# Two norms of the second layer whose sums of squares are taken later among the products

## The chip, the core and the metric

The kernel runs on one core of a Trainium2 chip. A core has engines that each work through a queue of their own in order and wait for one another by semaphores: TensorE (PE in the profile, with its weight loads as PEld) multiplies matrices into PSUM, VectorE (DVE) and ScalarE (ACT) do elementwise work, GpSimd (POOL) has very little to do here, and SyncE (SP) issues the transfers. The metric is the device time of one execution in microseconds (us); lower is better.

## What is computed

Two layers of a hybrid trunk over 256 latent tokens (LAT) with 256 context tokens (CTX), model width 1024. Cut to what the change touches:

```python
for l in range(DEPTH):                      # DEPTH = 2
    h  = modulate(rmsnorm(x,  norm1_g[l]), sh1, sc1)      # first norm, latent half
    hc = modulate(rmsnorm(xc, norm1_g[l]), csh1, csc1)    # first norm, context half
    p  = h @ w_in[l]                        # GLU columns, q, k, v, gates
    ...                                     # conv branch, attention, gated merge
    x  = x + g1 * gated_merge(...)
    h2 = modulate(rmsnorm(x, norm2_g[l]), sh2, sc2)       # second norm
    x  = x + g2 * conv_ffn(h2, w_up[l], ffn_dw[l], ffn_dw_b[l], w_down[l])
```

In the last layer (l = 1) the context gives only keys and values, and the feed-forward part runs over the latent tokens alone.

## The kernel before, in words

Activations lie with channels on the 128 partitions: `x[k]`, k = 0..7, is 128 channels by 512 tokens (256 latent, 256 context). Every weight tile of 128x1024 is fetched by a transfer (`raw`), split by ScalarE into a high part (`whi`, L160) and by VectorE into the rest (`wlo`, L161), with four buffers of each. A product of one weight tile is `mm3`: three matmuls, high weight by high activation (L179), high by low (L180), low by high (L181). One accumulation group is eight such triples, 24 matmuls, into one PSUM bank; there are two banks `sc`, four `main`, one `pt` and one `po`.

**A norm** has these steps. After each residual add (`x`, L898) the new `x[k]` is squared (ScalarE, L318) and added to a running sum `ss` (VectorE, L322). When all eight are in, TensorE sums `ss` over the partitions (`rstd`, L336, into `pt`); VectorE scales the result (`red`, L344); GpSimd raises it to the power -0.5 (`rs`, L346); TensorE spreads `rs` over the partitions (L351, into `po`). Then `modulated` runs for each k: VectorE multiplies x by gain and `po` (L365), ScalarE adds the shift and rounds to the high part (`h`, L366), and VectorE makes the low part (`h`, L367).

**Slots.** Side work is written as generators kept in a list; `slot()` is called between groups of matmuls and lets each generator take one step. `norm(..., rest)` is such a generator: it first rests for `rest` slots, then does L336 and `red` in one slot, waits one slot, does L351 and k = 0, 1 in the next, and two more k in each slot after that. A slot therefore sets where L336 and L351 stand in TensorE's queue; a scheduler then orders the other engines' queues by it.

**The first norm of layer 1** is made in two halves at the end of layer 0's down-projection: the latent half first, then the context half, with `rest` 1. The slots in which the context half runs are those at the start of layer 1: two per GLU weight tile (two tiles, banks `sc`), then one after each of the two groups of `glu_groups(1)` (banks `main`), then one after every second k of the V products (L644). V's first half uses the latent tokens, its second half is the first reader of the context half.

**The second norm of layer 1** does not run as side work. The four first up-projection tiles are multiplied by the un-normalised activations (258 columns: 256 tokens and two shift columns), row by row: row k is four tiles by three matmuls, 12 matmuls into banks `sc`, `sc`, `main`, `main`. Between rows, the code takes the first step of `sums` (L336, `red`, `rs`) and then the rest of it (L351). After row 7 `modulated` is written for all k, `po` is copied (`rstd1`, L1010), and the four products are multiplied by it (`u`, L1015), which frees their banks. The up-projections that follow are pairs i = 2..21, each two groups of 24 matmuls over the normalised `h2`, and each followed by `ffn_out`, which on VectorE is L964, L967 (twice each), L979 and L990.

Of the kernel before, what the change touches and what calls it, by code (L numbers as in the profile page):

```python
# [34 lines left out]
BADA, N1G, DW, DWB, LNG, LNB, N2G, FDW, FDB, NPAR = 0, 48, 56, 180, 184, 188, 192, 200, 332, 376  # L35
# [10 lines left out]
def trunk(ctx: ExitStack, tc: tile.TileContext, xt, cvec, crow, wall, wada, params, bias_t, rope_t, out):  # L46
# [19 lines left out]
    def psum(tag="main"):  # L66
        return psp.tile([P, 512], F32, tag=tag, bufs=BANKS[tag], name=nm(tag))
# [4 lines left out]
    def small(shape, tag, bufs=2):  # L72
        return tp.tile(shape, F32, tag=tag, bufs=bufs, name=nm(tag))
# [7 lines left out]
    def add_side(gen):  # L81
        side.append(gen)

    def slot():
        for g in list(side):
            try:
                next(g)
            except StopIteration:
                side.remove(g)

    def whole(g):

        while True:
            try:
                next(g)
            except StopIteration as e:
                return e.value

    def finish(g):
        for _ in g:  # L100
            pass
        if g in side:
            side.remove(g)
# [66 lines left out]
    def wunit(l, u, at=None, cuts=1):  # L170
        w, more = wparts(l, u, at, cuts)
        more()
        return w

    def cols(w, i):
        return sl(w[0], i), sl(w[1], i)

    def mm3(ps, w, xh, xl, start, stop):
        pe.matmul(ps, w[0], xh, start=start, stop=False)  # L179
        pe.matmul(ps, w[0], xl, start=False, stop=False)  # L180
        pe.matmul(ps, w[1], xh, start=False, stop=stop)  # L181
# [107 lines left out]
    def gain(l, part, off, k, ns=2):  # L289

        if (l, part) not in gains:
            gains[l, part] = cp.tile([P, KD, 2], F32, name=f"gain{l}_{part}")
        a = gains[l, part][:, k, :ns]
        g = pr(l, off + k, 1).to_broadcast([P, ns])
        dve.scalar_tensor_tensor(a, mod2(l, part, k)[:, :ns], 1.0, g, ALU.add, ALU.mult)
# [29 lines left out]
    def sum_squares(n, T, apart=False):  # L325

        at = tp.tile([P, 512], F32, tag="ss", name=nm("ss"))
        return [SumSq(T, at[:, i * T : (i + 1) * T], apart) for i in range(n)]

    def rstd(ss, n, bank):  # L330

        nt = ss.T // P
        pt = psum("pt")
        for i, p in enumerate(ss.parts):
            for t in range(nt):
                pe.matmul(  # L336
                    pt[:, t : t + 1], sl(p, t), one, start=i == 0 and t == 0, stop=i == len(ss.parts) - 1,
                    skip_group_check=True,
                )
        return (yield from root(pt, nt, n, bank))  # L340
# [13 lines left out]
    def h_tiles():  # L354
        return [[hp.tile([P, 2 * S + 2], F32R, tag=f"h{i}{k}", name=nm("h")) for k in range(KD)] for i in range(2)]

    def modulated(l, pb, scale, shift, k, h, streams):

        hi, lo = h[0][k], h[1][k]
        y = tmp()  # L360
        for s in streams:
            c = slice(s * S, (s + 1) * S)
            o = (s - streams[0]) * S
            a, b = gains[l, scale][:, k, s : s + 1], mod(l, shift, k, s)
            dve.scalar_tensor_tensor(y[:, c], x[k][:, c], a, pb[:, o : o + S], ALU.mult, ALU.mult)  # L365
            high = act.activation(hi[:, c], y[:, c], AF.Identity, bias=b)  # L366
            low = dve.scalar_tensor_tensor(lo[:, c], y[:, c], b, hi[:, c].bitcast(F32), ALU.add, ALU.subtract)  # L367
        return high, low

    def norm(l, acc, scale, shift, goff, h, streams, rest=0):  # L370
        for _ in range(rest):
            yield
        pb = yield from rstd(acc, D, "po")
        for k in range(KD):
            if streams[0] == 0:
                gain(l, scale, goff, k, 1 if l == DEPTH - 1 and scale == 4 else 2)
        for k in range(KD):
            modulated(l, pb, scale, shift, k, h, streams)
            if k % 2:
                yield  # L380
# [175 lines left out]
    h1 = h_tiles()  # L556

    for l in range(DEPTH):
# [5 lines left out]
        with ExitStack() if last else start as e1a:  # L564
# [68 lines left out]
            with ExitStack() as e1b:  # L633
# [98 lines left out]
                else:  # L732
                    sp.dma_start(rope, rope_t)
                    pg0 = [psum("sc") for _ in range(2)]
                    for uu in range(2):
                        wg = wunit(l, U_GLU0 + uu)
                        for i in range(2):
                            for kk in range(4):
                                k = 4 * uu + kk
# [76 lines left out]
            with ExitStack() as e1c:  # L816
# [79 lines left out]
                def residual(ss_, ps, part, n, s, off):  # L896
                    c = slice(s * S, (s + 1) * S)
                    dve.scalar_tensor_tensor(x[n][:, c], ps[:, off : off + S], mod(l, part, n, s), x[n][:, c], ALU.mult, ALU.add)  # L898
                    ss_.add(x[n][:, c], n == KD - 1)
# [19 lines left out]
                sss = sum_squares(NS, S)  # L919
# [15 lines left out]
                for s in range(NS if held else 0):  # L935
# [8 lines left out]
                    if s == 0:  # L944
                        finish(g1)
                        nl = norm(l, sss[0], 4, 3, N2G, h2, (0,))
# [3 lines left out]
        with ExitStack() as e2:  # L950
            ef = e2.enter_context(tc.tile_pool(name=f"ef{l}", bufs=1))
            if not last:
                finish(nl)
                nl = norm(l, sss[1], 4, 3, N2G, h2, (1,))
# [41 lines left out]
            if last:  # L996

                with tc.issue_after(lastev[0].ins):
                    act.activation(small([P, 1], "mx"), one, AF.Silu)
                for k in range(KD):  # L1000
                    for w, ps in zip(first, pss):
                        mm3(ps[:, : S + 2], w[k], h2[0][k][:, RAW], h2[1][k][:, RAW], k == 0, k == KD - 1)
                    if k == 2:
                        next(sums)
                    if k == 4:
                        pb = whole(sums)
                for k in range(KD):
                    modulated(l, pb, 4, 3, k, h2, (0,))
                rb = ef.tile([P, 512], F32, name="rstd1")
                act.copy(rb[:, LAT], pb[:, LAT])  # L1010
                for i, ps in enumerate(pss):
                    b = small([P, 1], "wb", 4)
                    act.copy(b, ps[:, S : S + 1])
                    u = ef.tile([P, S], F32, name=f"u{l}_{i}")
                    dve.tensor_tensor(u, ps[:, LAT], rb[:, LAT], ALU.mult)  # L1015
                    act.activation(u, u, AF.Identity, bias=b)
                    pss[i] = u
            else:
                for k in range(KD):
                    for w, ps in zip(first, pss):  # L1020
                        mm3(ps[:, LAT], w[k], h2[0][k][:, LAT], h2[1][k][:, LAT], k == 0, k == KD - 1)
                    slot()
                finish(nl)
# [29 lines left out]
            if not last:  # L1053
                h1 = h_tiles()
            sss = sum_squares(NS, S, last)
# [7 lines left out]
            for streams, ns in [((0, 1), range(NB)), *(((s,), range(NB, KD)) for s in range(NS))]:  # L1063
                wu = None
                c = slice(streams[0] * S, (streams[-1] + 1) * S)
                for n in ns:
                    ps = psum()
                    for k in range(KF):
                        t = n * KF + k
                        if t % 8 == 0 or not wu:  # L1070
                            wu = wunit(l, U_DN + t // 8)
                        mm3(ps[:, c], cols(wu, t % 8), fh[k][:, c], fl[k][:, c], k == 0, k == KF - 1)
                        if k % 4 == 3:
                            slot()
                    for s in streams:
                        residual(sss[s], ps, 5, n, s, s * S)
                    if last:
                        scaled = act.mul(x[n][:, CTX], x[n][:, LAT], par[:, DEPTH * NPAR + n : DEPTH * NPAR + n + 1])
                        if n == KD - 2:
                            with tc.issue_after(scaled.ins):  # L1080
                                act.activation(small([P, 1], "wb", 4), one, AF.Sqrt)
                if not last and streams == (0,):
                    finish(ad)
                if not last and len(streams) == 1:
                    nl = norm(1, sss[streams[0]], 1, 0, N1G, h1, streams, streams[0])
                    add_side(nl)


# [136 lines left out]
```

## Time and profile before

| | |
|---|---|
| median of 3 runs | 1131.16 us (1129.35 to 1134.31) |
| profiled execution, its own time | 1129.86 us |
| span of that execution, first to last instruction | 1128.1 us |
| mean granted TensorE clock | 0.997 |
| moved by transfers | 190.83 MB, mean 169 GB/s |

The difference between the span and the execution's own time, 1.8 us, lies around the first and the last instruction. In the tables of the profile, times are in us from the span's start; the two matmuls of L336 are listed there as four rows ("x4"). A bracket at the end of a timeline row is the idle time of that engine just before the row and what ended it. The TensorE clock and DMA share in the last columns of the table of windows are shares of full.

### The profile page before, as it was taken

What the parts mean: (1) busy time and instruction counts of PE and PEld (TensorE: products, weight loads), DVE (VectorE), ACT (ScalarE), POOL (GpSimd) and SP (SyncE); (2) the same over time, 40 slices, a digit from 0 to 9 for tenths busy, and PEclk for the clock granted to TensorE, in tenths of its full rate; (3) what the DMA queues carried; (4) which work ended last, traced back from release to release, by engine and by line L of the source; (5) the groups of instructions that cost most, each with busy time, mean ns of one, the idle gap of its engine ahead of it and who ended that gap; (6) DMA issues with size and microseconds to landing.
All of it is one profiled execution on the core that took longest, in us unless ns stands there. A gap on an engine that the chain in (4) does not pass through costs nothing.

```text
span 1128.1 us, 17731 instructions
## 1 busy us (share of the span) xinstructions
PE 1113.2 (99%) x6828; PEld 963.1 (85%) x6828; DVE 909.4 (81%) x1631; ACT 563.3 (50%) x934; POOL 17.2 (2%) x24
## 2 busy tenths in 40 slices
PE   9999999999999999999999999999999999999997
PEld 6778777787789988888888888989898999999997
DVE  5689999685778788888898555789996898988773
ACT  4347657542333543434443223444677567766642
POOL 0000000000000000000000000000000000000000
PEclk9999999999999999999999999999999999999998
DMA  9823231636734344554556655545433575565771
GB/s 361 283 94 104 75 117 38 205 97 217 245 114 144 114 154 149 168 172 146 172 171 218 224 185 189 175 174 175 153 121 115 181 240 172 187 194 180 217 269 57
DMA packets 53941, 190.83 MB, mean 169 GB/s; under 512 B 6240, under 2 KB 6496, under 8 KB 53856
## 3 DMA queue, kind: packets, MB, share of 16 engines
q1 hardware_dynamic: 53568, 189.65, 51.6%
q8 instruction: 54, 0.88, 0.3%
q14 instruction: 31, 0.25, 0.1%
q10 hardware_dynamic: 288, 0.04, 0.0%
HBM read 188.62 MB, written 1.05 MB: 168 GB/s over the span
## 4 chain that ended last, share of the span: by engine, by line
PE 84%; DVE 10%; DMA 3%; ACT 2%; issue 1%; SPq 0%; DVEq 0%; ACTq 0%
PE main L179 25%; PE main L181 24%; PE main L180 24%; DVE cb L591 4%; PE main L644 4%; DVE wlo L161 2%; DMA raw<-in_wall 1%; PE sc L179 1%; PE sc L181 1%; PE sc L180 1%; PE po L202 1%; PE po L512 1%; DMA x<-in_xt 1%; DMA sb<-in_crow 0%; PE sc L440 0%
## 5 line engine op out<-in xcount | busy, mean ns | idle before, releaser
L179 PE MATMUL main<-h,whi 128*128 128x256 f32 (+1 forms) x1328 | 447.5, 338 | 0.0
L181 PE MATMUL main<-h,wlo 128*128 128x256 f32 (+1 forms) x1328 | 444.0, 335 | 0.5 <-DVE wlo L161 0.5
L180 PE MATMUL main<-h,whi 128*128 128x256 f32 (+1 forms) x1328 | 443.0, 334 | 0.0
L160 ACT CAST whi<-raw 128x1024 fp32r<-128x1024 f32 (+1 forms) x244 | 252.4, 1039 | 286.0 <-PE main L180 127.3
L161 DVE TENSOR_TENSOR wlo<-raw,whi 128x1024 fp32r<-128x1024 f32 (+1 forms) x244 | 293.5, 1209 | 113.9 <-ACT whi L160 107.3
L179 PEld LDWEIGHTS main<-h,whi 128*128 128x128 f32 x1328 | 249.8, 188 | 31.8 <-issue 3.9
L181 PEld LDWEIGHTS main<-h,wlo 128*128 128x128 f32 x1328 | 250.0, 189 | 28.7 <-DVE wlo L161 0.7
L180 PEld LDWEIGHTS main<-h,whi 128*128 128x128 f32 x1328 | 250.3, 189 | 27.9 <-issue 0.2
L591 DVE SCALAR_TENSOR_TENSOR cb<-u,par,cb 128x512 f32<-128x512 f32 (+1 forms) x240 | 140.4, 617 | 1.2
L271 DVE CUSTOM_DVE_ANT_0 t<-raw,sb,par 128x1024 bf16<-128x1024 f32 x100 | 126.8, 1279 | 1.0 <-ACT sb L255 0.8
L180 PE MATMUL main<-fl,whi 128*128 128x256 f32 (+1 forms) x386 | 123.1, 319 | 0.0
L179 PE MATMUL main<-fh,whi 128*128 128x256 f32 (+1 forms) x386 | 123.1, 319 | 0.0
L181 PE MATMUL main<-fh,wlo 128*128 128x256 f32 (+1 forms) x386 | 123.1, 319 | 0.0
L180 PEld LDWEIGHTS main<-fl,whi 128*128 128x128 f32 x386 | 72.8, 189 | 5.6
L181 PEld LDWEIGHTS main<-fh,wlo 128*128 128x128 f32 x386 | 72.8, 189 | 5.5
L179 PEld LDWEIGHTS main<-fh,whi 128*128 128x128 f32 x386 | 72.8, 189 | 5.5
L963 ACT ACTIVATE t<-main,par 128x512 f32<-128x512 f32 (+1 forms) x82 | 50.6, 668 | 40.0 <-PE main L181 39.8
L964 DVE SCALAR_TENSOR_TENSOR t<-main,par,t 128x510 f32<-128x510 f32 (+1 forms) x82 | 47.6, 616 | 10.5 <-ACT t L963 10.1
L967 DVE SCALAR_TENSOR_TENSOR t<-main,par,t 128x510 f32<-128x510 f32 (+1 forms) x82 | 46.6, 611 | 0.0
L366 ACT ACTIVATE h<-t,mod 128x256 fp32r<-128x256 f32 x56 | 25.2, 501 | 35.8 <-DVE t L365 35.8
L898 DVE SCALAR_TENSOR_TENSOR x<-main,mod,x 128x256 f32<-128x256 f32 x48 | 22.1, 480 | 23.4 <-PE main L181 23.2
L644 PE MATMUL main<-whi,h 128*128 128x512 f32 x128 | 40.5, 402 | 0.1
(221 smaller groups left out, 1193.1 us busy)
## 6 DMA issues: line engine op xcount, KB each, us to landing
raw<-in_wall SPq DMA_DIRECT2D x239, 512.0 KB, 4.2
raw<-in_wada SPq DMA_DIRECT2D x88, 512.0 KB, 4.4
bias<-in_bias_t SPq DMA_DIRECT2D x8, 640.0 KB, 4.3
row<-in_wada SPq DMA_DIRECT2D x8, 512.0 KB, 5.1
sb<-in_crow SPq DMA_DIRECT2D x5, 512.0 KB, 5.7
x<-in_xt SPq DMA_DIRECT2D x8, 256.0 KB, 4.1
raw<-in_wall SPq DMA_DIRECT2D x8, 256.0 KB, 7.3
out<-t SPq DMA_DIRECT2D x3, 256.0 KB, 2.1
```

Source lines behind the costliest of these rows:

```text
L160: act.copy(hi[:, c], r[:, c])
L161: dve.tensor_tensor(lo[:, c], r[:, c], hi[:, c].bitcast(F32), ALU.subtract)
L179: pe.matmul(ps, w[0], xh, start=start, stop=False)
L180: pe.matmul(ps, w[0], xl, start=False, stop=False)
L181: pe.matmul(ps, w[1], xh, start=False, stop=stop)
L271: dve.tensor_tensor_reduce(tmp().bitcast(BF16), r, v, 1.0, pr(l, BADA + n, 1), ALU.mult, ALU.add, mods[l][:, n, s : s + 1])
L366: high = act.activation(hi[:, c], y[:, c], AF.Identity, bias=b)
L591: dve.scalar_tensor_tensor(cb[j], src, w, cb[j], ALU.mult, ALU.add)
L644: mm = pe.matmul(pv[t], h1[n == 1][k][:, c], w[n == 2][:, b], start=k + n == 0, stop=k == KD - 1 and n == 2)
L963: act.activation(c, pv_, AF.Identity, bias=pr(l, FDB + t, 1), scale=w[1])
L964: dve.scalar_tensor_tensor(c[:, :, 1:], pv_[:, :, : S - 1], w[0], c[:, :, 1:], ALU.mult, ALU.add)
L967: dve.scalar_tensor_tensor(c[:, :, : S - 1], pv_[:, :, 1:], w[2], c[:, :, : S - 1], ALU.mult, ALU.add)
```

## The change

Two places of the second layer are edited. The context half of the first norm rests three slots instead of one (`3 * streams[0]` is 0 for the latent half, as before). In the second norm, the two steps of `sums` stand after rows 4 and 6 instead of after rows 2 and 4.

```diff
                 for k in range(KD):
                     for w, ps in zip(first, pss):
                         mm3(ps[:, : S + 2], w[k], h2[0][k][:, RAW], h2[1][k][:, RAW], k == 0, k == KD - 1)
-                    if k == 2:
+                    if k == 4:
                         next(sums)
-                    if k == 4:
+                    if k == 6:
                         pb = whole(sums)
...
                 if not last and len(streams) == 1:
-                    nl = norm(1, sss[streams[0]], 1, 0, N1G, h1, streams, streams[0])
+                    nl = norm(1, sss[streams[0]], 1, 0, N1G, h1, streams, 3 * streams[0])
                     add_side(nl)
```

No instruction is added or removed. What moves is shown at three places. In the rows, `sc`, `main`, `pt`, `po` are PSUM banks, and a number behind a name is only a running number.

TensorE at the start of layer 1, before: L336 of the context half stands after the first GLU weight tile.

```order
L180 MATMUL sc_6520<-h_5453,whi_6522 128x256
L181 MATMUL sc_6520<-h_5445,wlo_6523 128x256
L336 MATMUL pt_6551<-one,ss_5458 128x1 x2
L179 MATMUL sc_6519<-h_5446,whi_6559 128x256
L180 MATMUL sc_6519<-h_5454,whi_6559 128x256
```

The same place in the change: L336 stands after the second GLU weight tile, ahead of the first group in a `main` bank.

```order
L180 MATMUL sc_6520<-h_5457,whi_6552 128x256
L181 MATMUL sc_6520<-h_5449,wlo_6553 128x256
L336 MATMUL pt_6581<-one,ss_5458 128x1 x2
L179 MATMUL main_6591<-h_5442,whi_6593 128x256
L180 MATMUL main_6591<-h_5450,whi_6593 128x256
```

L336 has moved 24 matmuls later. L351, which stood at the point where L336 stands now, has moved 48 matmuls later, to just ahead of the first product for V (L644).

TensorE after the row products of layer 1's second norm, before: the pair i = 2 begins, and its first group (`main_9203`) runs through k = 0, 1, 2, ... by itself.

```order
L179 MATMUL main_9203<-h_8305,whi_9192 128x256
L180 MATMUL main_9203<-h_8313,whi_9192 128x256
L181 MATMUL main_9203<-h_8305,wlo_9193 128x256
L179 MATMUL main_9203<-h_8306,whi_9192 128x256
L180 MATMUL main_9203<-h_8314,whi_9192 128x256
L181 MATMUL main_9203<-h_8306,wlo_9193 128x256
```

The same place in the change: the two groups of the pair (`main_9203` and `main_9228`) are mixed from the start.

```order
L179 MATMUL main_9203<-h_8305,whi_9192 128x256
L179 MATMUL main_9228<-h_8305,whi_9198 128x256
L180 MATMUL main_9203<-h_8313,whi_9192 128x256
L181 MATMUL main_9203<-h_8305,wlo_9193 128x256
L179 MATMUL main_9203<-h_8306,whi_9192 128x256
L180 MATMUL main_9228<-h_8313,whi_9198 128x256
L180 MATMUL main_9203<-h_8314,whi_9192 128x256
```

Ahead of these rows, L336 and L351 of this norm have each moved 24 matmuls (two rows of k) later, so that 12 matmuls instead of 36 stand between L351 and the pair i = 2.

VectorE in the up-projections, before: `wlo_9525`, the low weight part for the first group of pair i = 6, stands right behind the product of i = 0 (`t_9348`).

```order
L161 TENSOR_TENSOR wlo_9455<-raw_9453,whi_9454 128x1024
L990 TENSOR_TENSOR fl_3_9340<-t_9334,fh_3_9339 128x256
L979 TENSOR_TENSOR t_9348<-t_9348,t_9343 128x256
L161 TENSOR_TENSOR wlo_9525<-raw_9523,whi_9524 128x1024
L990 TENSOR_TENSOR fl_0_9354<-t_9348,fh_0_9353 128x256
```

VectorE at the same place in the change: the same row stands behind the work of i = 4 and i = 1.

```order
L967 SCALAR_TENSOR_TENSOR t_9433<-u_3_9188,par,t_9433 128x255
L967 SCALAR_TENSOR_TENSOR t_9438<-u_2_9183,par,t_9438 128x255
L990 TENSOR_TENSOR fl_4_9430<-t_9424,fh_4_9429 128x256
L979 TENSOR_TENSOR t_9438<-t_9438,t_9433 128x256
L161 TENSOR_TENSOR wlo_9525<-raw_9523,whi_9524 128x1024
L990 TENSOR_TENSOR fl_1_9444<-t_9438,fh_1_9443 128x256
```

Twelve VectorE instructions that followed `wlo_9525` now stand ahead of it: eight of the kinds L964 and L967, two L979 and two L990. The order of SyncE and GpSimd is the same in both kernels.

## The prediction

> **What bounds the kernel now.** I read the page first, then who TensorE waits for, then the timeline at the two norms.
>
> ```profile
> span 1128.1 us, 17731 instructions
> PE 1113.2 (99%) x6828; PEld 963.1 (85%) x6828; DVE 909.4 (81%) x1631; ACT 563.3 (50%) x934; POOL 17.2 (2%) x24
> PE 84%; DVE 10%; DMA 3%; ACT 2%; issue 1%; SPq 0%; DVEq 0%; ACTq 0%
> PE pt L336 <- DVE ss L322: 3.4, 2, 1.9
> PE main L181 <- DVE wlo L161: 0.5, 1, 0.5
> ```
>
> The first two rows are the span and the busy times, the third is the chain of waits by engine, the last two are from the table of waits of TensorE (us in total, times, longest). TensorE is busy 99% of the span and carries the chain. Its largest wait is for the sums of squares at L336: two waits, 3.4 us, and they are the two that the change moves. More than about 3.6 us (0.3%) cannot come out of removing them. Everything else must come from what the moved rows delay.
>
> **First norm, context half: what is removed.**
>
> ```profile
> 733.98 1.05 ACT L160 CAST whi<-raw 128x1024 fp32r<-128x1024 f32 x1 [3.85 <-DMA raw<-in_wall]
> 734.57 0.28 PE L181 MATMUL sc<-h,wlo 128*128 128x256 f32 x1
> 736.20 0.42 DVE L322 TENSOR_TENSOR ss<-ss,t 128x256 f32<-128x256 f32 x1
> 736.77 0.58 PE L336 MATMUL pt<-one,ss 128*128 128x1 f32 x4 [1.92 <-DVE ss L322]
> 737.70 1.67 POOL L346 TENSOR_TENSOR rs<-red,mhalf 128x2 f32<-128x2 f32 x1 [4.41 <-DVE red L344]
> 739.99 0.28 PE L181 MATMUL sc<-h,wlo 128*128 128x256 f32 x1
> 740.11 0.38 PE L351 MATMUL po<-ident,rs 128*128 128x128 f32 x2
> 740.52 0.87 DVE L365 SCALAR_TENSOR_TENSOR t<-x,gain,po 128x256 f32<-128x256 f32 x2 [1.71 <-PE po L351]
> 746.01 0.63 PE L644 MATMUL main<-whi,h 128*128 128x512 f32 x2
> 750.69 0.88 DVE L367 SCALAR_TENSOR_TENSOR h<-t,mod,h 128x256 fp32r<-128x256 f32 x2
> ```
>
> TensorE stops after 734.57 until the last addition to ss has run (736.20 to 736.62). The addition is late because ScalarE's cast, which stands ahead of the last square, waited for a transfer until 733.98. Matmuls start 0.119 apart (48 of them between 740.24 and 746.01 make 5.77 us), so without the wait TensorE stands at 734.69 where L336 stood, and 24 matmuls later, at 737.5, where it stands now. The sum is ready at 736.62, 0.9 us earlier. So the wait goes whole: 1.92 by the bracket, 2.08 by the starts; I take **2.0 us**.
>
> Behind it nothing becomes late. L351 moves to the place of the first L644, at 746.01 - 2.1 = 743.9, 3.8 us later than now, and rs is done about 3 us before that even if the power takes 1.67 us again. Context k = 0 is then ready some 3.8 us later than now, k = 7 (now ready at 751.57, the end of the row of 750.69) at about 755.4. The second half of V, the first reader, starts 48 matmuls of 0.23 behind the first L644, 11.2 us, so at 757.2 now and 755.1 then, and reads k = 7 only 42 such matmuls later. Both V tiles and keys are covered by several us.
>
> Whether the 2 us survive the attention stage is the first unknown, because VectorE is full there:
>
> ```profile
> 746.00:775.00 29.00, 29.00 (x155) 24.72 (x154) 28.59 (x60) 10.91 (x16) 0.00 (x0) 1.00 0.43 149
> 800.00:850.00 50.00, 50.00 (x370) 43.68 (x367) 49.63 (x127) 38.23 (x76) 0.84 (x1) 1.00 0.43 137
> 859.53 1.23 DVE L161 TENSOR_TENSOR wlo<-raw,whi 128x1024 fp32r<-128x1024 f32 x1 [2.00 <-PE pt L494]
> 866.76 0.42 DVE L519 TENSOR_TENSOR ol<-po,oh 128x256 fp32r<-128x256 f32 x1 [6.00 <-ACT oh L518]
> ```
>
> In the two windows (sum of busy, then PE, PEld, DVE, ACT, POOL, clock, transfers) VectorE has under 1.5% idle, but TensorE has none at all, and VectorE rests 2.0 and 6.0 us right after. It works off a store of convolution taps there and is not what TensorE waits for. Bounds of this term: all of it kept, -2.1, or all given back, 0. I take the near end, since no row shows TensorE waiting in these windows.
>
> **Second norm: what is removed, and what comes back.**
>
> ```profile
> 932.75 0.28 PE L181 MATMUL main<-h,wlo 128*128 128x258 f32 x1
> 934.07 0.42 DVE L322 TENSOR_TENSOR ss<-ss,t 128x256 f32<-128x256 f32 x1
> 934.54 0.61 PE L336 MATMUL pt<-one,ss 128*128 128x1 f32 x4 [1.52 <-DVE ss L322]
> 936.17 0.70 POOL L346 TENSOR_TENSOR rs<-red,mhalf 128x2 f32<-128x2 f32 x1 [47.29 <-DVE red L344]
> 936.64 1.23 DVE L161 TENSOR_TENSOR wlo<-raw,whi 128x1024 fp32r<-128x1024 f32 x1 [0.55 <-ACT whi L160]
> 937.98 0.38 PE L351 MATMUL po<-ident,rs 128*128 128x128 f32 x2
> 938.40 1.26 DVE L365 SCALAR_TENSOR_TENSOR t<-x,gain,po 128x256 f32<-128x256 f32 x3 [0.54 <-PE po L351]
> 942.55 0.28 PE L179 MATMUL main<-h,whi 128*128 128x256 f32 x1
> 944.44 0.89 DVE L367 SCALAR_TENSOR_TENSOR h<-t,mod,h 128x256 fp32r<-128x256 f32 x2 [0.18 <-ACT h L366]
> 945.91 0.74 DVE L1015 TENSOR_TENSOR u<-main,rstd 128x256 f32<-128x256 f32 x2
> 948.38 0.28 PE L179 MATMUL main<-h,whi 128*128 128x256 f32 x1
> ```
>
> I keep these clock times and leave the earlier gain out. One row of k is 12 matmuls, 1.45 us (three rows between 938.12 and 942.55 make 4.43). L336 would stand at 932.87 + 2.9 = 935.8, 1.3 us after the sum is ready (934.49): the wait of **1.55 us** goes. But L351 then stands at 935.8, plus 0.55 for L336 itself, plus 24 matmuls: 939.2, where it now stands at 937.98. So the wait was not idle for the norm: it let L336 run 1.2 us earlier than it now will. VectorE's work on the eight k takes from 938.40 to 945.33, 6.9 us, and now ends at 946.5.
>
> TensorE meanwhile ends row 7 earlier, at 942.55 - 1.55 = 941.0, and wants to be through the pair i = 2 after 5.83 us (942.55 to 948.38), at 946.8. The mixed order of the two groups uses matmuls of the second where the first must wait, but six matmuls stand behind the first use of the last k: 946.5 + 0.7 = 947.2 at best. Then pair i = 3 needs the bank that the third L1015 reads; now that is done (946.3) 1.0 us after the last L367, so then at 947.6. Pair 3 starts at 947.7 instead of 946.8: **0.9 us** come back (0.4 if only the six matmuls count, 1.5 if VectorE's rows also slip by the ScalarE copies L1013 between them).
>
> The second thing to come back is the low weight part of pair 6.
>
> ```profile
> 947.01 1.23 DVE L161 TENSOR_TENSOR wlo<-raw,whi 128x1024 fp32r<-128x1024 f32 x1 [0.35 <-ACT whi L160]
> 949.55 1.23 DVE L161 TENSOR_TENSOR wlo<-raw,whi 128x1024 fp32r<-128x1024 f32 x1 [1.32 <-ACT whi L160]
> 950.70 0.87 DVE L964 SCALAR_TENSOR_TENSOR t<-main,par,t 128x255 f32<-128x255 f32 x2
> 953.52 0.42 DVE L979 TENSOR_TENSOR t<-t,t 128x256 f32<-128x256 f32 x1
> 960.23 1.22 DVE L161 TENSOR_TENSOR wlo<-raw,whi 128x1024 fp32r<-128x1024 f32 x1
> 965.66 0.28 PE L181 MATMUL main<-h,wlo 128*128 128x256 f32 x1
> 949.00:1000.00 51.00, 51.00 (x434) 51.00 (x433) 46.61 (x84) 36.31 (x63) 0.00 (x0) 1.00 0.57 183
> 1000.00:1060.00 60.00, 60.00 (x510) 60.00 (x509) 50.15 (x85) 39.72 (x64) 0.00 (x0) 1.00 0.62 188
> ```
>
> This part is now made at 960.23 to 961.45 and first read at 965.66, 4.2 us later. In the change twelve instructions come ahead of it: eight like those of 950.70 (the second of two starts 0.39 after the first) and four like that of 953.52 (0.34 to the next), 4.5 us. VectorE is also 1.2 us late from the norm, and can make up part of that from the 0.35 and 1.32 us that it now rests; I take 0.55 late. The part is then done at 961.45 + 4.5 + 0.55 = 966.5. TensorE comes 0.7 us earlier than now, but has four matmuls instead of two ahead of that read: 965.66 - 0.7 + 0.24 = 965.2. It waits **1.2 us** (0 if VectorE catches up and casts keep pace, 2.4 if it stays 1.2 late and the next part, for the second group, waits behind it too). After that VectorE needs less than TensorE (50.15 of 60 us busy), so the delay does not grow.
>
> Second norm: -1.55 + 0.9 + 1.2 = **+0.5 us** (bounds -1.15 and +2.35). Both: -2.0 + 0.5 = **-1.5 us**, bounds -3.25 and +2.35. No instruction is added, so nothing else is priced. The profiled execution took 1129.86 us, of which 1128.1 are its span; it would become 1128.4. The median of the runs shown, 1131.16, lies 1.3 above that execution, and the same -1.5 gives **1129.7 us**.
>
> One row speaks for a longer chain: L346 took 1.67 us at 737.70, where VectorE ran a low weight part, and 0.70 us at 936.17, where the low part started after it. [...] In the change the second norm's power stands behind the low part of 936.64, with VectorE then idle, so I use 0.70; with 1.67, L351 would come about 0.5 us later and the sum would be -1.0.
>
> **The rivals.** (a) *Nothing comes back*: both waits vanish and pair 2's mixing and VectorE's slack hide the rest: -3.6, so 1127.6. For it: TensorE never waited for a low part in 949 to 1060. Against: the eight k end at 945.33 now with TensorE already on the seventh of them, so there was no slack to use up. (b) *Slower: VectorE's queue in the pairs i = 2 to 7 becomes the bound.* It is 1.2 us late from the norm and carries the products of i = 0 and 1 on top of i = 3 and 4. If the late parts are those of both groups of pair 6 (2.4 and 1.2 us) and the pair 2 waits cost 1.5, the second norm costs 5.1 - 1.55 = +3.55, and with -2.0 the kernel is 1.5 slower: 1132.7. It decides from 3.55 us of new waits on. Against it: VectorE has 4.4 us idle in 949 to 1000. (c) *The 2 us are given back in the attention stage*, where VectorE is full and its order changed: +0.5, so 1131.7. Against it are the 8 us of rest at 859 to 867. (d) *The waits only change their place*, L336 waiting as long for a sum that comes later with it: 0, so 1131.2. Against it: 0.9 and 1.3 us of margin at the new places.
>
> **How the numbers follow.** Forecast (-1.5, its own range -2.8 to -0.3) 0.55; (a) 0.12; (b) 0.18; (c) 0.12; (d) 0.03. The cases run from 1127.6 to 1132.7, the bounds from 1127.9 to 1133.5; runs of the kernel before scatter from 1.8 below to 3.1 above their median. The range 1126.3 to 1134.0 leaves out about 2 in 10. What can be told from no change is about 0.5%, 5.7 us. No removed wait reaches it: 0.06 for faster, for scatter on top of (a). Slower by that much needs (b) well beyond its price: 0.11. Within: 0.83.
>
> **What would show it.** In the changed profile L336 of both norms has no wait for ss; TensorE waits in fractions of a us at L180 within pair 2 and once, about 1 us, for wlo at the start of pair 6. The forecast is wrong if the table of waits has no such wait (then a), if waits on wlo in 945 to 975 exceed 3.5 us (b), or if TensorE waits between 746 and 906 where it now does not (c).

## The result, and the profile after

| | before | changed |
|---|---|---|
| median | 1131.07 us (11 runs) | 1127.69 us (11 runs) |
| lowest to highest | 1128.73 to 1134.31 | 1127.27 to 1128.88 |
| ratio of the two, 95% interval | | 0.9972 (0.9964 to 0.9981) |
| profiled execution, its span | 1129.86, 1128.1 | 1127.64, 1125.9 |

The change is faster by 3.4 us in the medians (2.1 to 4.1 by the interval), 0.3%, within the half per cent that the prediction set as "no change". The time lies in the predicted range, 2.0 us below the predicted 1129.7. Two things in the table are not in the prediction: the medians differ by 3.4 us, the profiled executions by 2.2; and the scatter has shrunk from 5.6 to 1.6 us.

The page of the changed kernel, in the order in which the page of the kernel before was shown: span, busy times, chain of waits by engine, and the two rows of TensorE's table of waits (us in total, times, longest) that are new or have grown.

```profile
span 1125.9 us, 17731 instructions
PE 1114.1 (99%) x6828; PEld 963.0 (86%) x6828; DVE 908.3 (81%) x1631; ACT 563.6 (50%) x934; POOL 14.7 (1%) x24
PE 83%; DVE 9%; issue 6%; ACT 2%; DMA 0%; POOL 0%; POOLq 0%; DVEq 0%; SPq 0%; ACTq 0%
PE main L181 <- DVE wlo L161: 1.0, 2, 0.6
PE po L351 <- POOL rs L346: 0.4, 1, 0.4
```

The row for ss at L336 (3.4 us) is gone from the table. In its place stand a wait of 0.4 us for rs and a second wait for a low weight part. The timeline of the changed kernel at the two norms shows where:

```profile
719.81 0.38 PE L351 MATMUL po<-ident,rs 128*128 128x128 f32 x2
737.07 0.50 PE L336 MATMUL pt<-one,ss 128*128 128x1 f32 x4
743.20 0.38 PE L351 MATMUL po<-ident,rs 128*128 128x128 f32 x2
743.34 0.71 PE L644 MATMUL main<-whi,h 128*128 128x512 f32 x2
886.44 0.38 PE L351 MATMUL po<-ident,rs 128*128 128x128 f32 x2
933.09 0.50 PE L336 MATMUL pt<-one,ss 128*128 128x1 f32 x4
934.84 1.23 DVE L161 TENSOR_TENSOR wlo<-raw,whi 128x1024 fp32r<-128x1024 f32 x1 [0.83 <-ACT whi L160]
935.98 0.15 DVE L344 TENSOR_SCALAR red<-pt 128x2 f32<-128x2 f32 x1
936.22 0.69 POOL L346 TENSOR_TENSOR rs<-red,mhalf 128x2 f32<-128x2 f32 x1 [49.93 <-DVE red L344]
936.97 0.43 PE L351 MATMUL po<-ident,rs 128*128 128x128 f32 x2 [0.40 <-POOL rs L346]
938.68 0.39 PE L179 MATMUL main<-h,whi 128*128 128x256 f32 x2
945.23 0.39 PE L179 MATMUL main<-h,whi 128*128 128x256 f32 x1
962.30 1.22 DVE L161 TENSOR_TENSOR wlo<-raw,whi 128x1024 fp32r<-128x1024 f32 x1
963.57 0.39 PE L181 MATMUL main<-h,wlo 128*128 128x256 f32 x1 [0.56 <-DVE wlo L161]
1116.70 0.50 PE L1094 MATMUL pt<-one,ss 128*128 128x1 f32 x4
```

Neither L336 has a bracket. At the second norm `red` stands behind a low part that waited for ScalarE, so rs was late and L351 stood 0.40. Pair i = 2 takes 945.23 - 938.68 = 6.55 where it took 5.83: its matmuls start up to 0.36 apart in five places, where 0.12 is usual. Pair i = 6 waits 0.56 for its low part.

The same landmarks of the kernel before that the prediction did not show:

```profile
720.23 0.38 PE L351 MATMUL po<-ident,rs 128*128 128x128 f32 x2
889.03 0.38 PE L351 MATMUL po<-ident,rs 128*128 128x128 f32 x2
1118.95 0.50 PE L1094 MATMUL pt<-one,ss 128*128 128x1 f32 x4
```

They cut the program into three stretches, which are used for every kernel below. **A** runs from the L351 of the first norm's latent half to the first product for V: before 746.01 - 720.23 = 25.78, changed 743.34 - 719.81 = 23.53, so 2.25 won. **B** is the attention stage from there to the L351 of the norm that follows it: 143.02 and 143.10, so 0.1 given back. **C** runs from there to the first L1094: 229.92 and 230.26, so 0.34 lost. Together 1.8; the other 0.4 of the 2.2 us lie ahead of the first edit, in code that is the same. The question left is where the medians have the other 1.2 us from, and why the changed kernel no longer scatters.

### The profile page after: what moved, and what is told of

Same layout as the page of the kernel before. It is cut to its first block, busy times and chain, and to the rows that moved or that the text cites. A ratio compares the mean times of both kernels' runs of the same rounds, so it can differ in the third digit from the quotient of the medians.

```text
span 1125.9 us, 17731 instructions
## 1 busy us (share of the span) xinstructions
PE 1114.1 (99%) x6828; PEld 963.0 (86%) x6828; DVE 908.3 (81%) x1631; ACT 563.6 (50%) x934; POOL 14.7 (1%) x24
## 4 chain that ended last, share of the span: by engine, by line
PE 83%; DVE 9%; issue 6%; ACT 2%; DMA 0%; POOL 0%; POOLq 0%; DVEq 0%; SPq 0%; ACTq 0%
PE main L179 24%; PE main L181 24%; PE main L180 24%; DVE cb L591 4%; PE main L644 4%; DVE wlo L161 1%; PE sc L181 1%; PE sc L179 1%; PE sc L180 1%; PE po L202 1%; PE po L512 1%; PE sc L129 1%; PE sc L440 0%; DMA sb<-in_crow 0%; PE sc L494 0%
## 5 line engine op out<-in xcount | busy, mean ns | idle before, releaser
L964 DVE SCALAR_TENSOR_TENSOR t<-main,par,t 128x510 f32<-128x510 f32 (+1 forms) x82 | 47.5, 615 | 10.2 <-ACT t L963 9.8
L967 DVE SCALAR_TENSOR_TENSOR t<-main,par,t 128x510 f32<-128x510 f32 (+1 forms) x82 | 46.6, 609 | 0.0
L644 PE MATMUL main<-whi,h 128*128 128x512 f32 x128 | 40.6, 402 | 0.1
```

The costliest lines, as they stand in the source:

```text
L644: mm = pe.matmul(pv[t], h1[n == 1][k][:, c], w[n == 2][:, b], start=k + n == 0, stop=k == KD - 1 and n == 2)
L964: dve.scalar_tensor_tensor(c[:, :, 1:], pv_[:, :, : S - 1], w[0], c[:, :, 1:], ALU.mult, ALU.add)
L967: dve.scalar_tensor_tensor(c[:, :, : S - 1], pv_[:, :, 1:], w[2], c[:, :, : S - 1], ALU.mult, ALU.add)
```

## The experiments

### The two edits apart

The first norm alone:

```diff
-                    nl = norm(1, sss[streams[0]], 1, 0, N1G, h1, streams, streams[0])
+                    nl = norm(1, sss[streams[0]], 1, 0, N1G, h1, streams, 3 * streams[0])
```

> Edit of the first norm alone (context half rests three slots; second norm as before). Theory A, the sum of the prediction: -2.0 us against the kernel before, and runs that scatter as widely as those of the kernel before (some 5 us). Theory B: the usual run of the kernel before waits longer at the first norm's L336 than the profiled one (1.92 us), since that wait ends with the landing of a transfer; then this edit alone gives the whole -3.4 us, and the runs lie within about 1.6 us as those of the changed kernel do. Theory C: the extra 1.4 us come from the second norm; then -2.0 here and a wide scatter.

Measured: 1128.77 us (12 runs, 1126.96 to 1132.48), ratio 0.9976 (0.9964 to 0.9989), so 2.7 us faster, but with a scatter of 5.5 us. Eight runs lie at 1126.96 to 1129.15 and four at 1130.52 to 1132.48. Theory B wanted a narrow scatter and falls. Theories A and C have the scatter right, and the interval (1.2 to 4.1 us faster) holds the -2.0 of both, so this run doesn't tell them apart.

The second norm was meant to be moved alone, and the first norm to rest two slots beside it. In both kernels that ran, both steps of the second norm stand behind row 6, so that L351 follows L336 after only a few matmuls; the numbers expected for rows 4 and 6 don't hold for them.

```diff
-                    if k == 2:
+                    if k == 6:
                         next(sums)
-                    if k == 4:
+                    if k == 6:
                         pb = whole(sums)
```

> Edit of the second norm alone (steps after rows 4 and 6; first norm as before). Theory A: +0.5 us against the kernel before. Theory B: +0.3 us or so, and runs that scatter as widely as before, with a wait of 1.9 us or more at the first norm's L336. Theory C: -1.4 us.

Measured: 1131.92 us (12 runs, 1129.27 to 1132.6), ratio 0.9998 (0.9987 to 1.0009). Five runs lie at 1129.27 to 1130.56 and seven at 1131.83 to 1132.6. The profiled one is the fastest, so what slows the seven was not seen.

> As the changed kernel, but the first norm's context half rests two slots: L336 stands 12 matmuls (1.45 us) later than before, not 24. Theory A (wait 2.0 us): 0.6 us of wait are left, so 0.6 us above the changed kernel. Theory B (usual wait 3 to 3.5 us): 1.5 to 2 us of wait are left, 1.5 to 2 us above the changed kernel, and its scatter is wide again.

Measured: 1129.57 us (11 runs, 1128.7 to 1130.67), ratio 0.9983 (0.9974 to 0.9992). In their profiles L336 of the first norm waits 1.01 us with one slot (first row) and 0.28 with two (second row):

```profile
735.36 0.58 PE L336 MATMUL pt<-one,ss 128*128 128x1 f32 x4 [1.01 <-DVE ss L322]
737.12 0.58 PE L336 MATMUL pt<-one,ss 128*128 128x1 f32 x4 [0.28 <-DVE ss L322]
```

Neither shows a wait of 3 to 3.5 us, or the 1.5 to 2 us that would be left of it with two slots, as theory B had it. The kernel with two slots, whose profile has no wait above 0.5 us at either norm, scatters 2 us.

### The kernel before once more

> The kernel before once more, for a second profile. Theory B: the first norm's L336 waits another time than 1.92 us, behind another time of the transfer that the cast ahead of it waits for; if the execution takes over 1130.5 us the difference to the first profile stands in that wait. Theory A and C: 1.9 us again, and a difference in the execution stands at other rows (C: at the second norm's L336, other than 1.52).

This execution took 1131.43 us. L336 of the first norm waits 1.71 us and that of the second 1.21, less than in the first profile, though the execution is 1.6 us longer. B and C put the difference into a longer wait; A left it open. The table of windows shows what none of them has; its last three columns are the granted clock, the transfers' share and GB/s. The kernel before, first profile:

```profile
739.00:740.00 1.00, 1.00 (x11) 1.00 (x10) 0.00 (x0) 0.00 (x0) 0.37 (x1) 1.00 0.94 385
740.00:741.00 1.00, 1.00 (x11) 1.00 (x10) 0.47 (x2) 0.77 (x1) 0.00 (x0) 1.00 0.79 311
```

The kernel before, this profile, first the timeline of TensorE and then the same table of windows:

```profile
737.21 0.58 PE L336 MATMUL pt<-one,ss 128*128 128x1 f32 x4 [1.71 <-DVE ss L322]
739.07 0.41 PE L179 MATMUL sc<-h,whi 128*128 128x256 f32 x1
739.28 0.41 PE L180 MATMUL sc<-h,whi 128*128 128x256 f32 x1
```

```profile
737.00:738.00 1.00, 0.79 (x7) 0.82 (x8) 0.17 (x2) 0.00 (x0) 0.00 (x0) 1.00 1.03 352
739.00:740.00 1.00, 1.00 (x7) 1.00 (x6) 0.26 (x1) 0.00 (x0) 0.81 (x1) 0.50 0.99 385
740.00:741.00 1.00, 1.00 (x7) 1.00 (x7) 0.00 (x0) 0.00 (x0) 0.00 (x0) 0.50 0.91 303
742.00:743.00 1.00, 1.00 (x11) 1.00 (x10) 0.48 (x2) 0.77 (x1) 0.00 (x0) 1.00 0.32 127
```

Behind the wait the granted clock falls to half: matmuls start 0.21 apart, not 0.12, and 7 fit into a us, not 11. By windows of half a us it lasts from 738.5 to 741.9, 3.4 us. Stretch A is 27.11 against 25.78 although its wait is shorter. The profile of the first edit alone (an execution of 1130.52) has the same behind L336 of the second norm (timeline, then windows):

```profile
933.74 0.61 PE L336 MATMUL pt<-one,ss 128*128 128x1 f32 x4 [1.91 <-DVE ss L322]
```

```profile
934.00:935.00 1.00, 1.00 (x10) 1.00 (x10) 1.00 (x2) 0.99 (x2) 0.00 (x0) 1.00 1.04 360
935.50:938.00 2.50, 2.50 (x13) 2.50 (x13) 1.23 (x1) 0.57 (x1) 0.62 (x1) 0.50 0.89 251
939.00:942.00 3.00, 3.00 (x28) 3.00 (x27) 2.91 (x8) 1.34 (x4) 0.00 (x0) 1.00 0.51 169
```

The second norm's L336 was not moved in that kernel, and its wait of 1.91 us is longer than the 1.52 of the first profile of before. This gave **theory D**: the waits cost more than their length. In a part of the executions a wait of this size is followed by 3.4 us at half clock, which cost 1.4 us more; the change takes away the waits, and with them this.

### Filling the wait instead of moving it

If D holds, the stretch at half clock goes when TensorE works through the wait, even at no use. The kernel before with its norms in place, and products of the identity ahead of L336 of the two waits:

```diff
-    def rstd(ss, n, bank):
+    def rstd(ss, n, bank, fill=0):
...
         pt = psum("pt")
+        for _ in range(fill):
+            pe.matmul(sl(pt, 1), ident, ident, start=True, stop=True)
...
-        pb = yield from rstd(acc, D, "po")
+        pb = yield from rstd(acc, D, "po", 8 if l == 1 and scale == 1 and streams == (1,) else 0)
...
-                sums = rstd(sss[0], D, "po")
+                sums = rstd(sss[0], D, "po", 9)
```

> The kernel before with both norms where they stood; ahead of L336 of the two waits TensorE gets products of the identity that nobody reads (eight matmuls of 128x128 in fp32, about 1.7 us, at the first norm; nine at the second, of which three run some 30 us earlier). [...] Then filling the stretch, though it adds work, removes it: no slice at half clock before 1110 us, all runs within about 2 us of one another and none above 1132, median 1130.4 (the low group of the kernel before, 1129.8, plus 0.6 for the three extra matmuls). Theory B and C, transfers that land at different times: the scatter stays some 5 us and the median is 1132.

Measured: 1131.03 us (11 runs, 1130.28 to 1132.02), ratio 0.9998 (0.9988 to 1.0008). The scatter is 1.7 us where the kernel before, run beside it, has 6.1 (1128.73 to 1134.82). Its profile (line numbers are two higher here) has the fill in the timeline, and full clock in the windows of both norms:

```profile
734.90 1.95 PE L335 MATMUL pt<-ident 128*128 128x128 f32 x16
736.88 0.61 PE L338 MATMUL pt<-one,ss 128*128 128x1 f32 x4
939.09 0.43 PE L353 MATMUL po<-ident,rs 128*128 128x128 f32 x2 [0.89 <-POOL rs L348]
```

```profile
734.00:744.00 10.00, 9.96 (x86) 9.77 (x85) 5.91 (x11) 5.87 (x9) 0.69 (x1) 1.00 0.74 251
930.00:945.00 15.00, 14.09 (x117) 13.69 (x117) 11.73 (x24) 8.90 (x19) 0.70 (x1) 1.00 0.73 237
```

All eleven runs have a mean clock of 0.997 or 0.998. Nothing ends earlier here than in the kernel before: L338 stands at 736.88 where L336 stood at 736.77, and stretch A is 25.73. So most of the scatter of the kernel before is neither that of transfers nor of the wait's length: it goes when TensorE is kept busy (1.7 us against 6.1). The median is 0.6 above D's 1130.4; in the profile L353 got a wait of 0.89 on rs that the expectation did not have. What the fill saves (the stretches at half clock) it pays for in added work and that wait.

### The second edit alone, and two other placements

```diff
-                    if k == 2:
+                    if k == 4:
                         next(sums)
-                    if k == 4:
+                    if k == 6:
                         pb = whole(sums)
```

> Edit of the second norm alone, with its two steps after rows 4 and 6. Theory D: only the first norm's wait can halve the clock; runs in two groups 1.4 us apart, the lower at 1129.5 to 1130.3 (the low group of the kernel before, 1129.8, plus 0.3), the upper near 1131.4, none above 1132.5; median 1130 to 1131.4. Prediction's sum: +0.5 against the kernel before without any grouping, 1132.

Measured: 1130.61 us (12 runs, 1128.72 to 1132.64), ratio 0.9994 (0.9983 to 1.0005). Seven runs lie at 1128.72 to 1130.7 and five at 1131.57 to 1132.64: two groups and a median as D expects, though the lower group is wider than its 1129.5 to 1130.3. The highest is 0.1 above D's limit, and it is the profiled one, which has a case that D had not named. Its clock is at half for two stretches on end, 736.8 to 743.6 (timeline, then windows):

```profile
736.73 0.93 PE L336 MATMUL pt<-one,ss 128*128 128x1 f32 x4 [1.82 <-DVE ss L322]
```

```profile
737.00:740.00 3.00, 3.00 (x15) 3.00 (x15) 1.36 (x2) 0.00 (x0) 1.67 (x1) 0.50 0.87 289
740.00:743.00 3.00, 3.00 (x17) 3.00 (x16) 0.00 (x0) 0.14 (x1) 0.00 (x0) 0.50 0.50 183
744.00:746.00 2.00, 2.00 (x20) 2.00 (x19) 2.00 (x4) 1.97 (x3) 0.00 (x0) 1.00 0.00 0
```

Stretch A is 28.76 here, 3.0 above that of the first profile of before: twice 1.5. Stretch C, with the edit, is 229.65 and has no wait on rs.

Steps after rows 3 and 5, with the first norm as in the changed kernel:

```diff
-                    if k == 4:
+                    if k == 3:
                         next(sums)
-                    if k == 6:
+                    if k == 5:
                         pb = whole(sums)
```

> First norm as in the changed kernel, second norm's steps after rows 3 and 5. From the changed kernel's profile the sum of squares is ready at 932.41 where L336 would stand at 931.64: a wait of 0.8 us there, which is too short to halve the clock (theory D), against 0.4 of wait on rs and some 0.6 in pair 2 that go. Theory D: within 0.5 us of the changed kernel's 1127.7, all runs within 2 us. Theory C: half the way back in scatter, 3 us.

Measured: 1128.33 us (9 runs, 1126.93 to 1130.2), ratio 0.9971 (0.9961 to 0.9981). The profiled execution, the slowest, waits longer than the 0.8 expected, and that was enough (timeline, then the window behind it):

```profile
934.33 0.61 PE L336 MATMUL pt<-one,ss 128*128 128x1 f32 x4 [1.45 <-DVE ss L322]
```

```profile
935.00:938.00 3.00, 3.00 (x15) 3.00 (x15) 2.10 (x3) 1.37 (x3) 0.21 (x1) 0.50 0.89 246
```

The other eight, 1126.93 to 1129.44, lie about those of the changed kernel; they were not profiled. In at least one of nine the expectation "too short to halve the clock" was wrong, because the wait was 1.45 us and not the 0.8 worked out from one profile, and the scatter of 3.3 us is wider than the 2 that D gave.

The first norm resting two slots, second norm as in the changed kernel:

```diff
-                    nl = norm(1, sss[streams[0]], 1, 0, N1G, h1, streams, 3 * streams[0])
+                    nl = norm(1, sss[streams[0]], 1, 0, N1G, h1, streams, 2 * streams[0])
```

> As the changed kernel, first norm's context half rests two slots. Theory D: 0.3 to 0.6 us of wait are left at L336, too short to halve the clock: 0.3 to 0.6 us above the changed kernel, all runs within 2 us. Theory B: 1.5 to 2 us above it, wide scatter.

Measured: 1127.86 us (6 runs, 1126.95 to 1129.52), ratio 0.9966 (0.9952 to 0.9979). L336 of the first norm waits 0.40 in its profile, and stretch A is 24.24, 0.7 above the changed kernel's, at full clock:

```profile
738.11 0.58 PE L336 MATMUL pt<-one,ss 128*128 128x1 f32 x4 [0.40 <-DVE ss L322]
```

Theory B is out; 0.2 us between the medians of this and the changed kernel says nothing. The six runs lie 2.6 us apart where D allowed 2. The profiled one is the slowest of them though it has no half clock; its L351 at the start of stretch A stands at 721.69 where the changed kernel's stands at 719.81. So some of the scatter lies ahead of both norms; its cause was not looked for.

### A longer wait, and the kernel before twice more

Steps after rows 0 and 2, first norm as in the changed kernel:

```diff
-                    if k == 4:
+                    if k == 0:
                         next(sums)
-                    if k == 6:
+                    if k == 2:
                         pb = whole(sums)
```

> First norm as in the changed kernel (rests three slots); second norm's steps after rows 0 and 2, so that L336 stands 11 matmuls earlier than in the kernel before and waits some 2.9 us instead of 1.55, and L351, 10 matmuls behind it, waits some 0.7 us for rs. Without any effect on the clock: 1.3 and 0.7 us above the low group of the kernel with the first edit alone (1127.0 to 1129.2, its middle 1128.5), 1130.5 us, profile at full clock. Theory D: nearly every execution has a window with 2 us or more without products, so the profile shows half clock from about 935 for 3.4 or 6.8 us, and the median is 1131.9 or above (1.4 us a window), few runs below 1131.

Measured: 1131.24 us, ratio 1.0010 (1.0001 to 1.0019) against a kernel before of 1130.19; ten executions lie at 1129.44 to 1132.5, and one of 2816.72 us is left out of the reading. The median misses D's limit by 0.7. The profiled execution has half clock, and a wait of 2.66 us instead of 2.9 (timeline, then windows):

```profile
932.03 0.61 PE L336 MATMUL pt<-one,ss 128*128 128x1 f32 x4 [2.66 <-DVE ss L322]
```

```profile
933.00:936.00 3.00, 2.92 (x14) 2.62 (x14) 1.66 (x3) 1.54 (x4) 1.52 (x1) 0.50 0.73 259
936.50:938.00 1.50, 1.50 (x15) 1.50 (x15) 1.50 (x5) 0.63 (x2) 0.00 (x0) 1.00 0.55 216
```

The half clock in the profile is what D said. But that execution took 1129.92 us, less than the 1130.5 expected without half clock, so the sum behind the expectation was too high, and the median of 1131.24 says little for or against D. "Nearly every execution" can't be told either: the mean clock of seven of the ten is 0.994 to 0.996 and that of three 0.997, but the profiled execution, which has one stretch at half clock, is one of the three.

> The kernel before a third time. Theory D: its time is 1129.6 plus or minus 1 if no slice before 1110 us is at half clock, 1.4 us more for each stretch of 3.4 us at half clock behind L336 of the first norm (737) or of the second (935), and no half clock anywhere else.

> The kernel before a fourth time, as the third: the time follows from the count of 3.4 us stretches at half clock behind the two L336.

Measured: 1130.0 us, at full clock in the windows read behind both waits (738 to 742 and 935 to 940), as D says; and 1132.27, with one stretch at half clock (737.5 to 740.9) behind the first norm's L336. D's time for one stretch is 1131.0 plus or minus 1, so this is 0.3 above. The faster of the two, timeline and window:

```profile
737.03 0.58 PE L336 MATMUL pt<-one,ss 128*128 128x1 f32 x4 [1.89 <-DVE ss L322]
```

```profile
738.00:740.00 2.00, 2.00 (x19) 2.00 (x18) 1.07 (x1) 0.00 (x0) 1.63 (x1) 1.00 0.88 344
```

The slower:

```profile
737.02 0.58 PE L336 MATMUL pt<-one,ss 128*128 128x1 f32 x4 [1.92 <-DVE ss L322]
```

```profile
738.00:740.00 2.00, 2.00 (x12) 2.00 (x11) 1.07 (x1) 0.00 (x0) 1.62 (x1) 0.50 0.85 313
```

The waits are the same to 0.03 us and L336 stands at the same time; one execution is slowed behind it and the other isn't. So it is not the wait's length alone that decides.

## Why the prediction was right, and what it missed

The stretches of the profiled executions, in us (A: first norm, B: attention, C: second norm to the last norm):

| kernel, its profiled execution | A | B | C | half clock behind |
|---|---|---|---|---|
| before, 1129.86 | 25.78 | 143.02 | 229.92 | none |
| before, 1130.0 | 25.74 | 142.99 | 229.57 | none |
| before, 1131.43 | 27.11 | 143.01 | 229.51 | first norm |
| before, 1132.27 | 27.33 | 143.01 | 230.19 | first norm |
| changed, 1127.64 | 23.53 | 143.10 | 230.26 | none |
| first edit alone, 1130.52 | 23.53 | 143.11 | 231.67 | second norm |
| second edit alone, 1132.64 | 28.76 | 143.01 | 229.65 | first norm, twice |
| rows 3 and 5, 1130.2 | 23.53 | 143.13 | 232.06 | second norm |
| rows 0 and 2, 1129.92 | 23.52 | 143.11 | 232.45 | second norm |
| two slots, 1129.52 | 24.24 | 143.05 | 229.63 | none |
| both steps behind row 6, one slot, 1129.27 | 24.86 | 143.00 | 230.75 | none |
| both steps behind row 6, two slots, 1129.62 | 24.13 | 143.01 | 230.75 | none |
| wait filled, 1131.01 | 25.73 | 143.00 | 230.92 | none |

- **First norm, -2.0.** Right, and a little small: A shows 2.25, in all four kernels with this placement (23.52 or 23.53). L336 has no wait left, and nothing behind it became late.
- **The 2 us survive the attention stage.** Right: B gives back 0.1. Rival (c), 2 us given back there, is refuted.
- **Second norm, +0.5.** Right as a sum at full clock, +0.34 in the first pair of profiles, with other parts: the wait gone (-1.55); L351 waiting 0.45 by the starts for rs, which the prediction had not listed (it moved `rs` along with L336, which leaves L351 1.1 us behind the end of `rs`, as in 936.87 to 937.98 of the kernel before, but `red` slipped behind a late low part; the power itself took 0.69, near the 0.70 chosen; in the two profiles L346 takes 0.69 to 0.71 on 128x2 each time but for the 1.67 at 737.70, and no run shows what made that one longer); pair 2 longer by 0.72 (0.9 predicted); the low part of pair 6 late by 0.7 by the starts (1.2 predicted). The later profiles put it lower: C is 229.51 to 230.19 in four executions of before, and 229.65 and 229.63 in two kernels with the edit where rs came in time. The four of before have a mean of 229.80, and against it the three kernels with the edit at full clock lie between -0.2 and +0.5: the second edit by itself is worth nothing that can be told at full clock.
- **The rivals.** (b), VectorE's queue as the bound, is refuted: its late parts cost TensorE 0.56 us in one place. (d) is refuted, since both waits are gone. (a) gave 1127.6, which is the median measured, but not by its mechanism: it says that nothing comes back, and 0.45 + 0.72 + 0.7 came back.
- **How near it came.** The time is inside the predicted range, but the gain of 3.4 us in the medians is not inside the forecast's own -2.8 to -0.3. The range holds it because it also covers rival (a) and the scatter of the runs. The mechanism is borne out by the pair of profiles (-2.2, of which -1.8 in the stretches), not by the median.
- **The step that failed** is "the median of the runs shown lies 1.3 above that execution, and the same -1.5 gives 1129.7". It takes what lies between an execution and the median as something that the change leaves alone, and it prices each wait at its length alone, as "More than about 3.6 us (0.3%) cannot come out" does too. What lies between is, for the most part, a further price of the two waits in the executions where the clock halves behind them, and the profiled execution had been one without. Worked out from the runs: of 70 runs of the kernel before whose clock is known, the 28 with a mean clock of 0.997 or 0.998 have a median of 1129.55, the 35 at 0.995 and 0.996 one of 1131.66, the 7 below that one of 1133.62. A stretch of 3.4 us at half clock takes 0.0015 off the mean clock (half of 3.41 in 1128). The sorting is rough: the mean also holds the half clock at the program's end (5.7 us of the span in the first profile of before, 5.4 in that of the changed kernel), and the five profiled executions with one stretch have means from 0.995 to 0.997. From the high-clock group to the changed kernel are 1.9 us, which agrees with the profiles (2.25 - 0.1 - 0.34 = 1.8). From it to the median before (1131.07) are 1.5 more: the stretches at half clock that the change removes. Together 3.4.

What is shown: half clock follows these waits in six of the thirteen profiles, and in the nine that were read from 730 to 1110 us it stands nowhere else there; it costs 1.3 to 1.6 us a stretch in A; it goes with the idle time whether that is moved away or filled; and with it goes most of the scatter. D's "window with 2 us or more without products" is shown by no run as a limit: in its place stand a stretch of 1.91 us behind which the clock halved and two of 2.36 us, one with half clock behind it and one without (last table). That the whole 1.5 us between the medians are this is worked out from the groups, not seen execution by execution. No placement tried beats the changed kernel by more than its scatter: two slots and rows 3 and 5 are the same within their intervals.

## What to carry to other kernels

TensorE was the bound here, and in some executions a wait of 1.7 to 1.9 us in A was followed by half clock that cost 1.3 to 1.6 us a stretch more; the first profile did not show it. So where TensorE is the bound, look at the granted clock in windows of a us behind each of its longest waits, and take a second profile when the runs scatter by more than the waits explain. If a wait can't be moved, try to keep TensorE busy through it with products that nobody reads: here the time became steadier (1.7 us of scatter against 6.1) and not shorter (1131.03 us against 1131.26). Shrinking the first norm's wait to 0.4 us did as much here as removing it (1127.86 us and 1127.69).

## What the runs showed of the hardware

Behind some waits the granted clock falls from full to half, and later it comes back. Both edges can be read from windows of half a us. The second profile of the kernel before, with a third place at the program's end, where TensorE does nothing:

```profile
738.00:738.50 0.50, 0.50 (x7) 0.50 (x6) 0.50 (x2) 0.00 (x0) 0.36 (x1) 0.96 0.54 197
738.50:739.00 0.50, 0.50 (x4) 0.50 (x4) 0.50 (x1) 0.00 (x0) 0.50 (x1) 0.50 0.86 270
741.50:742.00 0.50, 0.50 (x5) 0.50 (x5) 0.00 (x0) 0.00 (x0) 0.00 (x0) 0.63 0.74 303
1124.00:1124.50 0.50, 0.00 (x0) 0.00 (x0) 0.50 (x3) 0.00 (x0) 0.00 (x0) 0.67 0.00 0
```

A mean of 0.96 over half a us means half clock for its last 0.04, so the clock falls at 738.46; 0.63 means half clock for the first 0.37, so it comes back at 741.87, 3.41 us later. Read in the same way, the stretch of the execution of 1132.27 runs from 737.46 to 740.88, 3.42 us, and the one of the second edit alone from 736.80 to 743.62, 6.82 us, twice 3.41. The 0.67 puts a last fall at 1124.17.

The table has each wait of over 1 us at L336. "Free" is the time from the end of the last product's row to the start of the first product behind L336. Edges with one decimal are read from the distance of the matmuls' starts (0.21 instead of 0.12); those of the first edit alone lie within the windows named.

| profile | wait | free from, to | free | half clock |
|---|---|---|---|---|
| rows 0 and 2 | 2.66 | 929.37, 932.50 | 3.13 | 932.9 to 936.3 |
| second edit alone | 1.82 | 734.91, 737.52 | 2.61 | 736.80 to 743.62 |
| first edit alone | 1.91 | 931.83, 934.20 | 2.37 | from 935.0:935.5 to 938:939 |
| before, 1132.27 | 1.92 | 735.10, 737.46 | 2.36 | 737.46 to 740.88 |
| before, 1131.43 | 1.71 | 735.51, 737.65 | 2.14 | 738.46 to 741.87 |
| rows 3 and 5 | 1.45 | 932.88, 934.79 | 1.91 | 934.9 to 938.3 |
| before, 1129.86 | 1.92 | 734.85, 737.21 | 2.36 | no |
| before, 1132.27 | 1.87 | 934.73, 937.07 | 2.34 | no |
| before, 1130.0 | 1.89 | 735.14, 737.47 | 2.33 | no |
| before, 1129.86 | 1.52 | 933.03, 935.01 | 1.98 | no |
| before, 1130.0 | 1.29 | 933.16, 934.92 | 1.76 | no |
| before, 1131.43 | 1.21 | 934.91, 936.59 | 1.68 | no |
| both steps behind row 6, one slot | 1.01 | 734.35, 735.80 | 1.45 | no |

In these profiles the clock halved behind all three stretches of 2.37 us or more, behind none of the three of 1.76 us or less, and behind three of the seven from 1.91 to 2.36 us. The fall does not come at a fixed time: it stands 1.9 us (second edit alone) to 3.5 us (rows 0 and 2) behind the start of the free stretch, in the first of these ahead of the first product. What decides between 1.91 and 2.36 us, as between the first norm's waits of 1.89 and 1.92 us in the third and the fourth profile of before, was not shown.
